# Modulation rows summed over features on VectorE and over partitions by a block of ones, in place of column-tiled products of the raw weights

## The chip, the cores and the metric

The kernel runs on one core of a Trainium2 chip. The metric is the device time of one execution in microseconds (us), as the median of three runs. The names of the engines in the rows are PE (TensorE, matrix products), PEld (its loads of the stationary operand), DVE (VectorE), ACT (ScalarE), POOL (GpSimd) and SP (SyncE, which here issues the transfers).

## The reference

Two networks run one behind the other on a sequence of 256 tokens of 1024 features. The first has two layers of three attention branches, which are merged by gates. The second has two layers as well, an even one (Fourier mixing and gated chunks, latent and context tokens) and an odd one (neighbourhood attention), each followed by a convolutional feed-forward network. All weights are fp32.

Only one piece of it is computed in another way by the change: the modulation rows of the second network. Two vectors, one for the latent tokens and one for the context, go through `silu` and are multiplied by a weight of 1024 x 6144 in each layer:

```python
s_lat = jax.nn.silu(c)
s_ctx = jax.nn.silu(c_ctx)
for layer in range(DEPTH):
    mod = (s_lat @ ada_w[layer] + ada_b[layer])[:, None, :]
    mod_c = s_ctx @ ada_w[layer] + ada_b[layer]
    sh1, sc1, g1, sh2, sc2, g2 = jnp.split(mod, N_MOD, axis=-1)
    csh1, csc1, cg1, csh2, csc2, cg2 = jnp.split(mod_c, N_MOD, axis=-1)
    h = modulate(x, norm1_g[layer], sh1, sc1)
    ...
    x = x + g1 * y
    x = x + g2 * conv_ffn(modulate(x, norm2_g[layer], sh2, sc2), ...)
```

In the last layer the context tokens are not carried on; there only the shift and scale of the first norm (the first two of the six parts) are used for the context.

## The kernel before

Weights come in pieces of 512 KB. `piece` (L163 to L176) loads one into a `raw` buffer by a transfer on SP's queue, ACT makes the upper half `whi` of each number (L173), and DVE the rest, `wlo` (L174). A product with a weight is three matmuls, upper by upper, upper by lower and lower by upper (`tok_target` L228 to L230, `feat_target` L238 to L240). The pieces go round in a ring of three raw buffers and seven pairs of halves (`rings = [(wp, 3, 7)]`).

Each engine works its instructions in one fixed order. A scheduler makes that order when the program is built, from modelled times, so the instructions of an engine don't stand there in the order of the source.

The modulation rows are made by a generator, `ada` (from L376), which the other stages call for a step at a time through `fill` (L181), two steps at once. There are two layers, six groups of 1024 columns in each, and eight steps `k` in a group. Each step loads a tile of 128 features x 1024 columns, `adaw`. It multiplies the tile as it is (raw fp32) by the two vectors `cs`, which are the stationary operand of 128 x 2: four products of 256 columns each, placed side by side in the array by `tile_position` (L392). The eight steps of a group add up in one PSUM bank. Then four DVE instructions of 2 x 256 add the bias (`adab`, L398), and four transfers write the rows to DRAM, into `modd`. The rows of layer 0 are made while the first network runs, those of layer 1 during the feed-forward network of layer 0. The last group of layer 1 is loaded at the end of the odd stage into buffers that are free by then (`adar`), multiplied at its end by `fill(1000)` (L1338), and its bias is added in the last feed-forward network. `load_mod` (L863) and `load_gates` (L873) fetch rows back from `modd`.

In the first network the large products have three PSUM banks, `ps_mm` with `turn = [None]`, since `ps_x` holds the fourth for the modulation sums; afterwards they have four.

Norms: `Row.rstd` (L299 to L315) makes the factor of a row, `xs` (L320) is the scaled row tile, `pT` its transposes on PE (L336), `hf` (L342, L346) applies the gain, and `hh` (L351) and `hl` (L353) are the halves that the next products read. At the boundary of the two layers of the first network the residual addition is `x_sb<-pw` (L778).

In the feed-forward network (`ffn`, from L1089) an iteration makes a tile of `pfg` (gate) and `pfv` (value), DVE makes `fg` from them (L1144), and `pfd` is the second product. `fill` is called once in every iteration there.

## Time and profile before

| what | us |
|---|---|
| median of three runs | 1633.25 (1631.62 to 1634.20) |
| profiled execution | 1632.92 |
| its span | 1631.0 |
| PE busy | 1603.7 (98%) |
| loads of the stationary operand | 1333.0 (82%) |
| DVE busy | 1035.2 (63%) |
| ACT busy | 797.5 (49%) |
| moved by transfers | 265.83 MB, mean 163 GB/s |

The profile is one execution, recorded by the hardware. Busy time is summed over the whole span, so a share says nothing of a single stage. Records of PE overlap: matmuls are pipelined and their ends are modelled. "Granted clock" is the share of TensorE's full clock that was given in a stretch. The chain of waits goes back from the last instruction, at each step to what released it or to the instruction ahead of it on its engine. An fp32 product leaves two records of matmuls, so a step of `ada` has eight of them.

### The profile page before, as it was taken

How to read it: one execution, taken by the hardware profiler on the slowest of the kernel's cores; microseconds unless marked ns; L12 is line 12 of the kernel's file. 1: busy time of each engine (PE TensorE's matmuls, PEld its weight loads, DVE VectorE, ACT ScalarE, POOL GpSimd, SP SyncE). 2: the span in 40 equal slices, each digit the busy share in tenths (PEclk: the TensorE clock that was granted, in tenths of full speed). 3: DMA queues.
4: the chain of work that ended last, by engine and by line, in shares of the span. 5: the costliest groups of instructions: out<-in, count | busy, mean ns of one | idle time of the engine just before them, and what ended most of it. 6: DMA issues, size and time to landing. Idle time of an engine off the chain costs nothing.

```text
span 1631.0 us, 25920 instructions
## 1 busy us (share of the span) xinstructions
PE 1603.7 (98%) x10017; PEld 1333.0 (82%) x10017; DVE 1035.2 (63%) x2133; ACT 797.5 (49%) x1353; POOL 29.7 (2%) x45
## 2 busy tenths in 40 slices
PE   7999999999999999999999999999999999999999
PEld 5878898977788989878897778777787777689897
DVE  6795556667866566785665553545448656688773
ACT  6465545455555455664363331333246554676451
POOL 0000000000000000000000000000000111100000
PEclk9999999999999999999999999999999999999999
DMA  7754565656655555542235562455424323566650
GB/s 270 234 182 145 197 222 175 202 200 207 205 163 188 195 182 169 165 149 83 73 104 181 181 188 85 161 176 173 125 78 134 101 59 117 184 223 229 221 168 27
DMA packets 79308, 265.83 MB, mean 163 GB/s; under 512 B 9744, under 2 KB 14672, under 8 KB 79184
## 3 DMA queue, kind: packets, MB, share of 16 engines
q1 hardware_dynamic: 79184, 264.17, 49.9%
q8 instruction: 79, 1.29, 0.3%
q14 instruction: 45, 0.37, 0.1%
HBM read 262.98 MB, written 1.15 MB: 162 GB/s over the span
## 4 chain that ended last, share of the span: by engine, by line
PE 89%; DVE 4%; DMA 3%; ACT 3%; issue 1%; SPq 0%; ACTq 0%; DVEq 0%
PE pfg L238 4%; PE pfg L240 4%; PE pfv L240 4%; PE pfg L239 4%; PE pfv L239 4%; PE pfv L238 4%; PE pfd L1162 4%; PE pfd L1164 4%; PE pfd L1163 4%; PE pmg L238 3%; PE pmg L240 3%; PE pmg L239 3%; PE pada L392 2%; DMA raw<-in_w_in 2%; DVE wlo L174 2%; PE poq L228 1%
## 5 line engine op out<-in xcount | busy, mean ns | idle before, releaser
L174 DVE TENSOR_TENSOR wlo<-raw,whi 128x1024 fp32r<-128x1024 f32 (+1 forms) x390 | 471.6, 1212 | 252.9 <-ACT whi L173 250.5
L173 ACT ACTIVATE whi<-raw 128x1024 fp32r<-128x1024 f32 (+1 forms) x390 | 406.9, 1049 | 408.3 <-PE pfd L1164 71.2
L238 PE MATMUL pfg<-hh,whi 128*128 128x256 f32 (+1 forms) x368 | 123.8, 337 | 1.9 <-ACT hh L351 1.9
L240 PE MATMUL pfg<-hh,wlo 128*128 128x256 f32 (+1 forms) x368 | 122.8, 334 | 0.0
L238 PE MATMUL pfv<-hh,whi 128*128 128x256 f32 (+1 forms) x368 | 121.5, 330 | 1.3 <-DVE fg L1144 1.3
L240 PE MATMUL pfv<-hh,wlo 128*128 128x256 f32 (+1 forms) x368 | 122.4, 333 | 0.0
L239 PE MATMUL pfg<-hl,whi 128*128 128x256 f32 (+1 forms) x368 | 121.9, 331 | 0.0
L239 PE MATMUL pfv<-hl,whi 128*128 128x256 f32 (+1 forms) x368 | 121.7, 331 | 0.0
L238 PE MATMUL pmg<-hh,whi 128*128 128x256 f32 x384 | 108.5, 282 | 0.0
L240 PE MATMUL pmg<-hh,wlo 128*128 128x256 f32 x384 | 107.6, 280 | 0.0
L239 PE MATMUL pmg<-hl,whi 128*128 128x256 f32 x384 | 107.6, 280 | 0.0
L1164 PE MATMUL pfd<-whi,gl 128*128 128x512 f32 (+1 forms) x275 | 105.8, 385 | 0.0
L1162 PE MATMUL pfd<-whi,gh 128*128 128x512 f32 (+1 forms) x275 | 105.7, 385 | 0.0
L1163 PE MATMUL pfd<-wlo,gh 128*128 128x512 f32 (+1 forms) x275 | 105.0, 382 | 0.0
L238 PEld LDWEIGHTS pfg<-hh,whi 128*128 128x128 f32 x368 | 69.6, 189 | 16.5 <-issue 3.9
L238 PEld LDWEIGHTS pfv<-hh,whi 128*128 128x128 f32 x368 | 69.2, 188 | 8.7 <-DVE fg L1144 1.5
L239 PEld LDWEIGHTS pfv<-hl,whi 128*128 128x128 f32 x368 | 69.6, 189 | 7.8
L239 PEld LDWEIGHTS pfg<-hl,whi 128*128 128x128 f32 x368 | 69.9, 190 | 7.2 <-DVE hl L353 0.2
L240 PEld LDWEIGHTS pfg<-hh,wlo 128*128 128x128 f32 x368 | 69.6, 189 | 7.0
L240 PEld LDWEIGHTS pfv<-hh,wlo 128*128 128x128 f32 x368 | 69.4, 188 | 7.0
L238 PEld LDWEIGHTS pmg<-hh,whi 128*128 128x128 f32 x384 | 72.2, 188 | 1.2 <-issue 1.2
L239 PEld LDWEIGHTS pmg<-hl,whi 128*128 128x128 f32 x384 | 72.2, 188 | 0.2 <-issue 0.2
(320 smaller groups left out, 3739.9 us busy)
## 6 DMA issues: line engine op xcount, KB each, us to landing
raw<-in_w_in SPq DMA_DIRECT2D x152, 512.0 KB
raw<-in_ffn_up SPq DMA_DIRECT2D x96, 512.0 KB
adaw<-in_ada_w SPq DMA_DIRECT2D x88, 512.0 KB
raw<-in_ffn_down SPq DMA_DIRECT2D x40, 512.0 KB
raw<-in_w_branch SPq DMA_DIRECT2D x24, 512.0 KB
raw<-in_odd_qkv SPq DMA_DIRECT2D x24, 512.0 KB
raw<-in_w_out SPq DMA_DIRECT2D x16, 512.0 KB
raw<-in_even_in SPq DMA_DIRECT2D x12, 512.0 KB
```

The costliest lines, as they stand in the source:

```text
L173: behind(ACT.activation(hi, raw, AF.Copy))
L174: behind((sub or DVE).tensor_sub(lo, raw, hi.bitcast(F32)))
L228: PE.matmul(ps, xh[:, k, tsl], hi, start=first, stop=False)
L238: PE.matmul(ps, hi[:, msl], xh[:, k, :], start=first, stop=False)
L239: PE.matmul(ps, hi[:, msl], xl[:, k, :], start=False, stop=False)
L240: PE.matmul(ps, lo[:, msl], xh[:, k, :], start=False, stop=last)
L392: PE.matmul(ps[32 * j:32 * j + 2, 0:256], cs[:, 2 * k:2 * k + 2], raw[:, j * 256:j * 256 + 256], start=k == 0, stop=k == KD - 1, tile_posi ...
L1162: PE.matmul(ps, gh[:, k, tsl], hi[:, i, csl], start=k == 0, stop=False)
L1163: PE.matmul(ps, gh[:, k, tsl], lo[:, i, csl], start=False, stop=False)
L1164: PE.matmul(ps, gl[:, k, tsl], hi[:, i, csl], start=False, stop=k == NH - 1)
```

## The change

Each step `k` no longer goes to PE. For each needed row `s`, DVE multiplies the whole tile of 128 x 1024 by the factor of each partition (`cs[:, 2k+s]`) and adds it to a sum `adaa`: a multiplication for k = 0, then seven multiply-adds. Two rows are made in layer 0 and in the first two groups of layer 1, one row in the other four. At a group's end PE adds the sum up over the partitions: the stationary operand is a block of 128 x 32 ones, the moving one is `adaa`, again in four column tiles of 256 columns, for each row. One DVE instruction adds the bias (`adar`, now spread over 32 partitions), and four transfers write the rows.

Counted over the program, DVE gets 20 multiplications and 140 multiply-adds of 128 x 1024 and 12 read-outs (eight of 128 x 512, four of 128 x 256), and loses 48 instructions of 2 x 256. On PE 96 groups of four products go, and 20 groups of four come, in 12 places (two groups in eight of them, one in four).

With it go: the separate bank (`ps_x`), so that the first network has the fourth bank as well; the preloaded last group of layer 1, which is now made in the feed-forward network of layer 0 like the others; one pair of the halves' buffers (seven to six); and `fill(2)` in the second half of that network becomes `fill(3)`.

```diff
-    turn = [None]
+    turn = [0]
...
-    rings = [(wp, 3, 7)]
+    rings = [(wp, 3, 6)]
...
+            rows_ = range(2 if layer == 0 or g < 2 else 1)
+            n = len(rows_)
+            acc = [pool.tile([P, 1024], F32, tag=f"adaa{s}", bufs=1, name=nm("adaa")) for s in rows_]
+            bias = pool.tile([P, 256], F32, tag="adab", bufs=1, name=nm("adab"))
             for j in range(4):
-                SP.dma_start(bias[32 * j:32 * j + 2, :],
-                             A["ada_b"][layer:layer + 1, s0 + j * 256:s0 + j * 256 + 256].broadcast_to([2, 256]))
-            ps = bank(nm("pada"))
+                SP.dma_start(bias[32 * j:32 * j + 32, :],
+                             A["ada_b"][layer:layer + 1, s0 + j * 256:s0 + j * 256 + 256].broadcast_to([32, 256]))
             for k in range(KD):
-                raw = ada_ahead.pop((g, k)) if (g, k) in ada_ahead else ada_load(layer, g, k)
-                for j in range(4):
-                    PE.matmul(ps[32 * j:32 * j + 2, 0:256], cs[:, 2 * k:2 * k + 2], raw[:, j * 256:j * 256 + 256],
-                              start=k == 0, stop=k == KD - 1, tile_position=(0, 32 * j))
+                raw = pool.tile([P, 1024], F32, tag="adaw", bufs=2, name=nm("adaw"))
+                SP.dma_start(raw, A["ada_w"][layer, g, :, k, :])
+                for s in rows_:
+                    c = cs[:, 2 * k + s:2 * k + s + 1]
+                    if k == 0:
+                        DVE.tensor_scalar_mul(acc[s], raw, c)
+                    else:
+                        DVE.scalar_tensor_tensor(acc[s], raw, c, acc[s], op0=ALU.mult, op1=ALU.add)
                 if k == KD - 1:
...
+                    ps = ps_tr(nm("pada"))
+                    for s in rows_:
                         for j in range(4):
+                            PE.matmul(ps[32 * j:32 * j + 32, s * 256:s * 256 + 256], C("ones", 0, 32),
+                                      acc[s][:, j * 256:j * 256 + 256], start=True, stop=True,
+                                      tile_position=(0, 32 * j))
+                    r = sp.tile([P, 2, 256], F32, tag="t512", bufs=4, name=nm("adar"))[:, 0:n, :]
+                    DVE.scalar_tensor_tensor(r, ps[:, 0:n * 256].rearrange("p (s c) -> p s c", s=n), 0.5,
+                                             bias.unsqueeze(1).broadcast_to([P, n, 256]), op0=ALU.mult, op1=ALU.add)
...
                 elif l == 0:
-                    fill(2)
+                    fill(3)
...
-        room = []
-        for tag in ("okT0", "okT1", "ov"):
-            r = po.tile([P, 2, 1024], F32, tag=tag, bufs=1, name=nm("adar"))
...
-        for k, r in enumerate(room):
-            ada_ahead[5, k] = ada_load(1, 5, k, r)
...
-        fill(1000)
```

On DVE at the start of the program, behind the first norm, stands before the change the following. `cs` are the vectors, `rope` and `qs` the turned heads, `wlo` a lower half of a weight.

```order
L812 SCALAR_TENSOR_TENSOR cs<-cs,vec 128x16
L423 TENSOR_TENSOR rope_284<-qs_282,cst 128x8x8
L424 TENSOR_TENSOR rope_284<-qs_282,cst 128x8x8
L425 TENSOR_TENSOR qs_282<-qs_282,cst 128x8x16
L426 TENSOR_TENSOR qs_282<-qs_282,rope_284 128x8x16
L174 TENSOR_TENSOR wlo_299<-raw_296,whi_298 128x1024
```

In the changed program the same place of DVE reads as follows.

```order
L804 SCALAR_TENSOR_TENSOR cs<-cs,vec 128x16
L383 TENSOR_SCALAR adaa_213<-adaw_220,cs 128x1024
L383 TENSOR_SCALAR adaa_214<-adaw_220,cs 128x1024
L385 SCALAR_TENSOR_TENSOR adaa_213<-adaw_224,cs,adaa_213 128x1024
L385 SCALAR_TENSOR_TENSOR adaa_214<-adaw_224,cs,adaa_214 128x1024
L415 TENSOR_TENSOR rope_281<-qs_279,cst 128x8x8
L416 TENSOR_TENSOR rope_281<-qs_279,cst 128x8x8
L171 TENSOR_TENSOR wlo_296<-raw_293,whi_295 128x1024
```

The first four sums stand ahead of the first `wlo` of the attention weights.

The next two pieces are DVE at the boundary of the two layers of the first network. Here `x_sb<-pw` is the residual addition of a row tile's half, `rsv`, `rsy` and `rst` the row factor, `xs` the scaled row. Before:

```order
L778 SCALAR_TENSOR_TENSOR x_sb<-pw_3814,x_sb 128x512
L309 SCALAR_TENSOR_TENSOR rsv_3868<-rss_3763,rsu_3764 128x1
L310 TENSOR_SCALAR rsv_3868<-rsv_3868 128x1
L174 TENSOR_TENSOR wlo_3863<-raw_3860,whi_3862 128x1024
L311 RECIPROCAL rsy_3870<-rsr_3869 128x1
L313 SCALAR_TENSOR_TENSOR rst_3871<-rsy_3870,rsv_3868 128x1
L314 SCALAR_TENSOR_TENSOR rsy_3870<-rst_3871,rsy_3870 128x1
L320 TENSOR_SCALAR xs_3878<-x_sb,rsy_3870 128x1024
L342 TENSOR_SCALAR hf_3881<-pT_3880,vec 128x128
L778 SCALAR_TENSOR_TENSOR x_sb<-pw_3904,x_sb 128x512
```

With the change, at the same boundary on DVE:

```order
L171 TENSOR_TENSOR wlo_3832<-raw_3829,whi_3831 128x1024
L306 SCALAR_TENSOR_TENSOR rsv_3837<-rss_3736,rsu_3737 128x1
L308 RECIPROCAL rsy_3839<-rsr_3838 128x1
L770 SCALAR_TENSOR_TENSOR x_sb<-pw_3873,x_sb 128x512
L307 TENSOR_SCALAR rsv_3837<-rsv_3837 128x1
L385 SCALAR_TENSOR_TENSOR adaa_3577<-adaw_4169,cs,adaa_3577 128x1024
L310 SCALAR_TENSOR_TENSOR rst_3840<-rsy_3839,rsv_3837 128x1
L306 SCALAR_TENSOR_TENSOR rsv_3901<-rss_3744,rsu_3745 128x1
L308 RECIPROCAL rsy_3903<-rsr_3902 128x1
L311 SCALAR_TENSOR_TENSOR rsy_3839<-rst_3840,rsy_3839 128x1
L307 TENSOR_SCALAR rsv_3901<-rsv_3901 128x1
L317 TENSOR_SCALAR xs_3847<-x_sb,rsy_3839 128x1024
```

The scaled row tile `xs` of the first row stood ahead of the last `x_sb<-pw`; now it stands behind it and behind a sum.

On PE, where the first attention scores (`psc`) begin, the order before has two steps of the modulation between a product and the scores:

```order
L229 MATMUL pq_979<-wlo_976,hh_90 128x512
L230 MATMUL pq_979<-whi_975,hl_91 128x512
L228 MATMUL pq_980<-whi_975,hh_90 128x512
L229 MATMUL pq_980<-wlo_976,hh_90 128x512
L230 MATMUL pq_980<-whi_975,hl_91 128x512
L392 MATMUL pada_218<-adaw_1043,cs 2x256 x4
L392 MATMUL pada_218<-adaw_1049,cs 2x256 x4
L499 MATMUL psc_1072<-qk_360 128x128
```

The same place of PE with the change:

```order
L225 MATMUL pq_969<-whi_964,hh_90 128x512
L226 MATMUL pq_969<-wlo_965,hh_90 128x512
L227 MATMUL pq_969<-whi_964,hl_91 128x512
L390 MATMUL pada_1040<-adaa_213,cst 32x256 x4
L390 MATMUL pada_1040<-adaa_214,cst 32x256 x4
L491 MATMUL psc_1064<-qk_357 128x128
```

It is the first visit of the modulation to PE in the changed program: the two row sums of group 0, where before it was one of several visits of group 0.

## Rows read from the trace of the kernel before

**Rows 1.** The page: busy time of the engines, DVE in 40 slices, chain by engine.
```profile
PE 1603.7 (98%) x10017; PEld 1333.0 (82%) x10017; DVE 1035.2 (63%) x2133; ACT 797.5 (49%) x1353; POOL 29.7 (2%) x45
...
DVE  6795556667866566785665553545448656688773
...
PE 89%; DVE 4%; DMA 3%; ACT 3%; issue 1%; SPq 0%; ACTq 0%; DVEq 0%
```

**Rows 2.** The chain of waits: start us, us, engine, name, line, count of records.
```profile
23.17 0.97 PE pada L392 x16
...
34.59 1.13 DVE wlo L174
...
392.00 1.14 DVE wlo L174
...
532.22 1.23 DVE wlo L174
...
879.74 0.98 PE pada L392 x16
892.11 0.97 PE pada L392 x16
```

**Rows 3.** Groups of PE and PEld by line and shape: busy us, mean ns | idle before.
```profile
L392 PE MATMUL pada<-adaw,cs 128*2 128x256 f32 x704 | 46.0, 379 | 0.0
...
L228 PEld LDWEIGHTS pq<-whi,hh 128*128 128x128 f32 x160 | 30.7, 192 | 8.7 <-issue 1.3 <-ACT hh L351 0.9
L392 PEld LDWEIGHTS pada<-adaw,cs 128*2 128x2 f32 x704 | 13.9, 83 | 22.3 <-issue 9.9 <-DMA raw<-in_w_in 0.7 <-DVE rope L424 0.4
```

**Rows 4.** Groups of DVE by line and shape, the same columns.
```profile
L174 DVE TENSOR_TENSOR wlo<-raw,whi 128x1024 fp32r<-128x1024 f32 x382 | 466.1, 1223 | 248.1 <-ACT whi L173 245.6 <-PE psg L1049 0.5
L398 DVE SCALAR_TENSOR_TENSOR adab<-pada,adab 2x256 f32<-2x256 f32 x48 | 20.1, 419 | 1.8 <-PE pada L392 0.8
...
L717 DVE SCALAR_TENSOR_TENSOR mth<-mth,py 128x512 f32<-128x512 f32 x16 | 10.9, 684 | 9.9 <-PE py L240 9.9
L320 DVE TENSOR_SCALAR xs<-x_sb,rsy 128x1024 f32<-128x1024 f32 x12 | 9.0, 754 | 0.4
L659 DVE MATCH_REPLACE8 wk<-m,wk 128x256 f32<-128x256 f32 x14 | 5.7, 408 | 0.0
L828 DVE SCALAR_TENSOR_TENSOR x_sb<-x_sb,rsy,fg 128x512 f32<-128x512 f32 x4 | 2.8, 749 | 0.1
```

**Rows 5.** Windows: us; PE, PEld, DVE, ACT, POOL busy; granted clock, DMA share, GB/s.
```profile
20.00:120.00 100.00, 98.84 (x586) 78.10 (x585) 80.95 (x215) 56.13 (x86) 0.00 (x0) 1.00 0.70 227
400.00:460.00 60.00, 59.38 (x370) 47.55 (x369) 50.66 (x139) 32.02 (x52) 0.00 (x0) 1.00 0.58 184
842.00:880.00 38.00, 38.00 (x239) 32.44 (x241) 22.73 (x27) 17.35 (x22) 0.00 (x0) 1.00 0.45 153
879.70:966.40 86.70, 86.70 (x453) 64.81 (x456) 46.32 (x60) 30.47 (x38) 0.00 (x0) 1.00 0.56 180
1039.50:1163.30 123.80, 123.80 (x645) 92.53 (x648) 63.16 (x80) 41.20 (x52) 0.00 (x0) 1.00 0.54 173
1437.00:1441.40 4.40, 4.07 (x20) 3.88 (x21) 3.12 (x6) 3.92 (x8) 0.00 (x0) 0.61 0.21 84
```

**Rows 6.** Timeline of PE at the boundary of the layers: start us, us, instruction.
```profile
353.21 0.40 PE L230 MATMUL pw<-whi,mh 128*128 128x512 f32 x1
...
354.97 0.50 PE L228 MATMUL pq<-whi,hh 128*128 128x512 f32 x1 [0.38 <-ACT hh L351]
```

**Rows 7.** Timeline of DVE at the same place.
```profile
351.24 0.75 DVE L320 TENSOR_SCALAR xs<-x_sb,rsy 128x1024 f32<-128x1024 f32 x1
...
353.92 0.68 DVE L778 SCALAR_TENSOR_TENSOR x_sb<-pw,x_sb 128x512 f32<-128x512 f32 x1
```

**Rows 8.** Timeline of PE behind the odd stage.
```profile
1434.34 1.06 PE L336 MATMUL pT<-cst,xs 128*128 128x128 f32 x8 [0.94 <-DVE xs L320]
1437.33 0.38 PE L238 MATMUL pfg<-hh,whi 128*128 128x256 f32 x1 [1.92 <-ACT hh L351]
```

## Prediction made before the changed kernel ran

> **What bounds the kernel now.** I read the page first. TensorE (PE) is busy 98% of the span, VectorE (DVE) 63%, and the chain of waits puts 89% of the span on PE and 4% on DVE [rows 1]. That says: time taken off PE comes off the end, unless the work that replaces it makes PE wait. The DVE line of the 40 slices shows where it could: mostly fives and sixes, but sevens, eights and a nine in slices 2 and 3 and at the end [rows 1]. Then I read the chain for the modulation products (L392). They stand in it 38 times, the first at 23.17 us, each visit of 16 matmul records (two k-tiles, four column tiles each, an fp32 product being two records) for 0.97 or 0.98 us, some for 1.02 [rows 2]; all visits together are 704 records, so 44 visits [rows 3]. These are visible stops of PE: in the feed-forward network of layer 0 one stands exactly every 12.37 us (879.74, then 892.11) [rows 2]. Last I read the windows of the places where the new DVE work will land, and there the idle of DVE: 19.05 of 100 us at 20 to 120, 9.34 of 60 us at 400 to 460, 15.27 of 38 us at 842 to 880 [rows 5].
>
> Times below are made against the profiled execution, 1632.92 us (span 1631.0). The median of the runs shown is 1633.25, 0.33 us more. Differences under 0.2%, 3.3 us, are about what a measurement of this kernel can tell from no change.
>
> **The change part by part.**
>
> *Taken from PE.* 38 visits on the chain at a mean of 0.975 us: 37.1 us. Six visits are not on the chain, worth 0 to 5.9 us; I take half, 2.9. The eight k-tiles of the last group, 64 records at 1428 to 1433 [rows 8], I count at nothing: the transposes of the next norm wait for `xs` behind them and the first `pfg` waits another 1.92 us for `hh` [rows 8], so DVE and ACT set the time there; were that cover gone, four more visits, 3.9 us, would be saved. Together -40.0.
>
> *Added to PE.* 20 products of four column tiles in 12 visits, eight with two rows (16 records) and four with one (8 records). The moving operand is again 128x256 in fp32, 379 ns a record, four column tiles side by side [rows 3]; the stationary one has 32 columns where it had 2. No row shows a 32-column load; the nearest are 83 ns for 2 columns and 192 ns for 128 [rows 3]. A visit of 16 records took 0.97 us, so by count 8x0.97 + 4x0.49 = 9.7 us. From above: 160 loads, each at 192 ns with no overlap, 30.7 us. From below the count stands: the same columns stream through as in the old visits, and nothing speaks for less. I take 9.7, as 32 columns lie nearer to 2 than to 128. Gross on PE: -30.3 (-6 to -33: the six visits left out and the loads in full, or the six counted in full).
>
> The Trainium skill ("TensorEngine Tiling (Array Packing)", Key Properties) says that changing the tiling mode drains TensorE, so that a price per visit would be right rather than one per product. By it the 12 visits would cost 12x0.97 = 11.7 instead of 9.7, 2 us more; no row here parts the two.
>
> *Added to DVE.* 20 multiplications and 140 multiply-adds of 128x1024 in fp32. The first kind is in the trace: 754 ns (`xs` L320) [rows 4]. The second is not at this width. The subtraction of the same shape with two sources takes 1223 ns; at 128x512 the multiply-add takes 749 (L828) and 684 (L717) ns [rows 4]. The dearer of these beside the cheaper gives 65 ns, so 1.288 us each (bounds 1.22 and 2x0.749 = 1.50). The 48 small `adab` instructions, 20.1 us, go [rows 4]; 12 read-outs of the ones products come, eight as long as the 128x512 of L717, 0.684 us, and four of half that width at 0.42, as long as an `adab` [rows 4]. Net: 15.1 + 180.3 + 7.2 - 20.1 = 182.5 us, DVE from 1035 to about 1218 us, 75% of the span. So DVE doesn't become the bound on the whole; it must be asked stretch by stretch. DVE works its instructions in the order in which they are written, so behind a sum stand the `wlo` halves that PE's products wait for.
>
> *Start, 20 to 120 us.* Ahead of the first attention output 21 sums now stand on DVE, four of them multiplications: 4x0.754 + 17x1.288 = 24.9 us. Two `wlo` (2.4 us), about eight selection instructions at 0.408 us (3.3) [rows 4] and about 1 us of `adab` left this stretch in exchange: net 18.2 against 19.05 us of idle [rows 5]. That is almost all of the idle, and some of it lies where DVE waits for a copy on ACT that in its turn waits for a transfer, hence is not free to use. Here the chain runs through `wlo` eight times, from 34.59 us on [rows 2]: PE is already waiting for DVE. Cost 0 to 18; I take 6, a third, because the scheduler puts the sums between the `wlo`, not in a block, while eight links of 1.1 to 1.2 us show that about a third of the added time can push directly.
>
> *Layer boundary, 352 us.* Before, the first row tile's `xs` (351.24) is done ahead of the last residual addition (353.92), so the transposes and the first `pq` of layer 1 are under way 1.4 us after the last `pw` product ended (353.61, `pq` at 354.97) [rows 6, 7]. In the new order of DVE two `wlo`, the last residual addition and one sum stand ahead of that `xs`. Then after the last `pw` come the addition 0.69, the sum 1.29, the small operations of the row factor (my estimate: 1.2, as `rsv` to `xs` is a chain of seven on columns of 128x1), `xs` 0.75, and as before some 3 us from `xs` to `pq` (351.24 + 0.75 to 354.97) [rows 6, 7]: 6.9 us instead of 1.4. That is 5.5 us. PE lost clock after an idle stretch before: at 1437 to 1441.4, behind the wait for `hh` [rows 8], the granted clock was 0.61 [rows 5], between its two levels of 0.5 (1.2 GHz) and 1 (2.4 GHz); 39% of 4.4 us is 1.7 more. I take 7 (3 if other PE work is in hand, 10).
>
> *Dense stretch of layer 1, 400 to 460 us.* 14 sums stand in it, 18.0 us, against 9.34 us of idle [rows 5]; but no link of the chain there is a DVE one (after the `wlo` at 392.00 the next in it is at 532.22 [rows 2]), so PE has work in hand. 0 to 8.7; I take 2.
>
> *Feed-forward network of layer 0.* 16 sums stand ahead of the fourth iteration's `fg`: 20.6 us against 15.27 us idle in 842 to 880 [rows 5], 5.3 short. Later in the first half an iteration has 46.32/7 = 6.6 us of DVE [rows 5], and four sums make 11.8, beside 12.37 - 0.97 = 11.40 us for PE. The `adab` share of 0.4 us in the 6.6 goes, so they are level. 0 to 5; I take 2. The second half has three sums in an iteration, 63.16/10 + 3.9 = 10.2 against 11.4 [rows 5]: nothing.
>
> *The rest.* Seven to six buffers for the weight halves, a fourth bank in block 1, stages that start 30 us of PE earlier with the same weights to load (DMA share 0.70 in the densest stretch [rows 5]), and the last group's sums in the feed-forward network instead of before the last one: 0, within 2 either way.
>
> Sum: -40.0 + 9.7 + 6 + 7 + 2 + 2 = -13.3, so 1619.6 us for the profiled execution, 1620 as median.
>
> **The rivals.**
>
> *All sums are covered.* DVE is idle 37% of the span [rows 1], and it is enough if the sums slip into gaps. Then the net is -27 to -33 and the time 1600 to 1606. For it: only 15 `wlo` links in block 1 are on the chain. Against it: the boundary, where the order itself puts `xs` behind a sum.
>
> *The sums block the weight halves (slower).* The mechanism is the order on DVE: a sum stands ahead of a `wlo` or `xs` that PE needs, and the idle before it was a wait for a copy or a transfer, which a queue can't use for something written further back. Then the idle of the dense stretches is worth nothing: 18 + 10 + 8.7 + 5 = 41.7 us come back, -30.3 + 41.7 = +11.4, 1645 us. It decides from 30.3 us of returned time, that is if three quarters of the overlap fails. For it: 248 us of DVE's idle is a wait for `whi` [rows 4]. Against: 38 of the 44 removed stops are real, and from 120 to 350 us DVE shows five and six tenths. The Trainium skill ("TensorE: Matmul & The Clock Gate", Architectural detail: the array is 16× 32×32, not 1× 128×128) calls VectorE's queue strict FIFO, which speaks for this rival; what it would make of the time is the 1645 of this paragraph, and the trace of before, with DVE on 4% of the chain, doesn't yet bear it out.
>
> *The products don't get cheaper.* If the ones products cost the upper 30.7 us, PE gains only 9.3, and with the same 17 us paid back the time is 1641. Against it: 16 records took under 1 us in a visit.
>
> **How the numbers follow.** Forecast with its neighbours (1606 to 1628): 0.45. All covered (1598 to 1606): 0.21. Between, within 0.2%, 1630 to 1636.5: 0.13 (this holds half of a partly blocked queue). Slower, by the queue or by the dear products: 0.21, of which half beyond 1642. So faster 0.66, same 0.13, slower 0.21. The range goes from 1602, which leaves half of the covered case below it, 0.1, to 1642, which leaves 0.1 above.
>
> **What would show it right or wrong.** After: 160 sums of about 1.29 us and 0.75 us, and 12 visits of at most 1 us on PE, no longer one per 12.37 us iteration; the iteration of the feed-forward network at 11.4 us. DVE busy near 1218 us. At the boundary of the layers `xs` behind the last `x_sb` addition, PE idle for 5 to 7 us with a lower granted clock after it. In 20 to 120 us more `wlo` links in the chain than eight. The forecast is wrong if PE's idle before `whi`/`wlo` products grows by more than 30 us in all, or if the iteration doesn't shrink because DVE's `fg` now ends last.

## The result and the profile after

The changed kernel takes 1610.78 us (median of four, 1609.79 to 1613.74) beside 1633.72 of the kernel before on the same chip: a ratio of 0.9862, with an interval of 0.9848 to 0.9877. Run once more, beside others, it gave 1611.32 us and 0.9868 (0.9853 to 0.9883). So it is 21 to 23 us faster; the forecast was 1620 us, in a range of 1602 to 1642. The profiled execution took 1610.21 us (span 1608.1).

The page of after, in the parts that answer to [rows 1]; the second line is DVE in 40 slices:

```profile
PE 1570.2 (98%) x9409; PEld 1328.9 (83%) x9409; DVE 1185.1 (74%) x2257; ACT 798.9 (50%) x1353; POOL 29.4 (2%) x45
...
DVE  7999668787987856876679784578558656688773
...
PE 85%; DVE 7%; DMA 4%; ACT 2%; issue 1%; SPq 0%; DVEq 0%; ACTq 0%
```

PE still carries the chain, but DVE's share went from 4% to 7%. The slices show where DVE filled up: slices 2 to 4, from 40 us on, are at 90% and more, where [rows 1] has 7, 9 and 5.

The answers for the tiles `adaa` and `pada` of after (count; shortest, median and longest ns; first and last start):

```profile
L385 DVE SCALAR_TENSOR_TENSOR adaa<-adaw,cs,adaa x140: 1251/1279/1287, 24.1 to 1131.2; 128x1024 f32<-128x1024 f32 x140
L383 DVE TENSOR_SCALAR adaa<-adaw,cs x20: 723/746/757, 22.8 to 1108.8; 128x1024 f32<-128x1024 f32 x20
...
L390 PEld LDWEIGHTS pada<-adaa,cst x160: 106/109/110, 103.1 to 1132.7; 128*32 128x32 f32 x160
```

A multiply-add takes 1.279 us (forecast 1.288), a multiplication 0.746 (0.754), and a load of 32 columns 109 ns, between the 83 and 192 of [rows 3].

The next table shows when the same matmul starts in the traces (us; the runs of the last four columns are told below; the traces of e2_short and e3_bound are of executions of 1603.72 and 1603.71 us, the shortest of theirs):

| matmul | before | after | e8_hybrid | e3_bound | e2_short | e10_split |
|---|---|---|---|---|---|---|
| first `ppT` (attention, layer 0) | 102.8 | 105.0 | 100.9 | 102.8 | 100.8 | 103.8 |
| 48th `pw` (end of layer 0) | 339.8 | 336.5 | 337.2 | 332.9 | 332.7 | 337.8 |
| 27th `psm` (start of layer 1) | 367.4 | 371.4 | 366.4 | 362.8 | 365.3 | 367.7 |
| first `pev` (second network) | 692.3 | 690.6 | 689.3 | 684.2 | 682.7 | 694.9 |
| first `pfg` (feed-forward, layer 0) | 830.6 | 827.5 | 826.3 | 821.2 | 820.0 | 831.8 |
| first `poq` (odd stage) | 1226.9 | 1205.5 | 1206.1 | 1199.1 | 1198.8 | 1210.2 |

The whole first network, with 24 of the 44 removed visits, gained 1.7 us (692.3 to 690.6). That is within what single executions differ by: a second trace of the changed kernel (e4_after_again) starts the first `pev` at 692.0, and the two traces of it already stand at 13.2 and 11.7 us at the ninth `pT`, ahead of the first sum (22.8 us). The feed-forward network of layer 0, with the other 20 visits, takes 396.3 us before (first `pfg` to first `poq`) and 378.0 in both traces of the changed kernel: 18.3 us gained (from 3.1 to 21.4 us ahead).

The other 2.9 us are 1.4 in the even stage and 1.5 in the last feed-forward network, most of them two waits of PE that the trace of before has and that of after has not:

```profile
722.79 0.50 PE L238 MATMUL pef<-hh,whi 128*128 128x512 f32 x1 [1.16 <-DVE vn L992]
...
1475.47 0.39 PE L238 MATMUL pfv<-hh,whi 128*128 128x256 f32 x1 [1.25 <-DVE fg L1144]
```

It doesn't take the new sums to lose them: e5_ring6, which is the kernel before with six pairs of the halves' buffers, has neither wait, though it keeps all products and every `adab`.

**The price of a visit.** The timeline of PE around one visit in the feed-forward network, before and then after (start us, us, instruction, count of records):

```profile
903.86 0.39 PE L239 MATMUL pfv<-hl,whi 128*128 128x512 f32 x1
904.09 0.40 PE L240 MATMUL pfv<-hh,wlo 128*128 128x512 f32 x1
904.42 1.05 PE L392 MATMUL pada<-adaw,cs 128*2 128x256 f32 x16
905.39 0.50 PE L238 MATMUL pfg<-hh,whi 128*128 128x512 f32 x1
905.73 0.39 PE L239 MATMUL pfg<-hl,whi 128*128 128x512 f32 x1
```

```profile
897.17 0.40 PE L237 MATMUL pfv<-hh,wlo 128*128 128x512 f32 x1
897.50 1.07 PE L390 MATMUL pada<-adaa,cst 128*32 128x256 f32 x16
898.50 0.50 PE L235 MATMUL pfg<-hh,whi 128*128 128x512 f32 x1
898.84 0.40 PE L236 MATMUL pfg<-hl,whi 128*128 128x512 f32 x1
...
1107.55 0.40 PE L237 MATMUL pfv<-hh,wlo 128*128 128x512 f32 x1
1107.87 0.64 PE L390 MATMUL pada<-adaa,cst 128*32 128x256 f32 x8
1108.44 0.50 PE L235 MATMUL pfg<-hh,whi 128*128 128x512 f32 x1
1108.78 0.39 PE L236 MATMUL pfg<-hl,whi 128*128 128x512 f32 x1
```

Matmuls of 512 columns start 0.23 us apart (903.86, 904.09). The visit starts 0.33 us after the one ahead of it, and the second matmul behind starts 0.34 after the first. From 904.09 to 905.73 are 1.64 us; two matmuls alone would be 0.47. So a visit costs 1.17 us, not the 0.97 of its own row in the chain. With two rows after it is 1.67 - 0.47 = 1.20, with one row 1.235 - 0.467 = 0.77: the two differ by one product, 0.43, and 0.34 is left for the visit itself. An iteration, 12.37 us before, is 11.2 now (46.0 us from the visit at 897.50 to that at 943.50 are four of them and one visit; the prediction's sign was 11.4).

**Covered in the feed-forward network.** Windows of after (us; busy PE, PEld, DVE, ACT, POOL; granted clock, DMA share, GB/s), first one in the feed-forward network, then the two places of the first network where PE waited:

```profile
898.80:943.30 44.50, 44.50 (x192) 35.66 (x190) 39.49 (x44) 15.12 (x19) 0.00 (x0) 1.00 0.58 184
...
80.00:90.00 10.00, 7.42 (x37) 5.23 (x36) 9.86 (x27) 7.27 (x10) 0.00 (x0) 0.74 0.71 226
340.00:362.00 22.00, 14.55 (x59) 11.59 (x58) 16.86 (x32) 11.90 (x29) 1.07 (x3) 0.77 0.56 186
```

With DVE busy for 39.5 of 44.5 us, 89%, PE didn't stop at all. At 80 to 90 us DVE is full (9.86 of 10 us) and PE stands for 2.6 us. At 340 to 362 us DVE is busy for less of the time than in the feed-forward network, 77%, and PE stands for 7 us. So how full DVE is doesn't decide it alone; what stands behind a sum in its queue does as well.

**The clock behind the waits.** Behind the waits for `pix` (2.58 us, told below) and for `xs` (6.88 us, in the next part) the granted clock falls. Two windows of after with the same columns, then the starts of PE in the second of them:

```profile
84.80:95.00 10.20, 9.41 (x27) 6.68 (x28) 8.30 (x28) 4.78 (x11) 0.00 (x0) 0.50 0.49 160
351.10:361.20 10.10, 5.65 (x21) 4.72 (x22) 7.62 (x21) 5.21 (x15) 0.34 (x1) 0.50 0.48 157
...
359.28 0.63 PE L227 MATMUL pq<-whi,hl 128*128 128x512 f32 x1
359.71 0.63 PE L225 MATMUL pq<-whi,hh 128*128 128x512 f32 x1
```

A share of 0.50 is the lower of the two levels, 1.2 GHz, and matmuls start 0.43 us apart there instead of 0.23. With 3.3 us more at 433 us PE was busy at it for 18.4 us, so by an estimate from these rows some 8 us of the first network are lost to the clock. From 15 to 692 us the kernel before and e8_hybrid have 1.00.

**The boundary of the layers.** DVE, then PE, in the timeline of after; the bracket is the idle time ahead of an instruction and what ended it:

```profile
348.26 1.28 DVE L385 SCALAR_TENSOR_TENSOR adaa<-adaw,cs,adaa 128x1024 f32<-128x1024 f32 x1 [2.06 <-DMA adaw<-in_ada_w]
349.47 2.35 DVE L171 TENSOR_TENSOR wlo<-raw,whi 128x1024 fp32r<-128x1024 f32 x2
...
351.88 0.67 DVE L770 SCALAR_TENSOR_TENSOR x_sb<-pw,x_sb 128x512 f32<-128x512 f32 x1
...
352.53 1.28 DVE L385 SCALAR_TENSOR_TENSOR adaa<-adaw,cs,adaa 128x1024 f32<-128x1024 f32 x1
...
354.17 0.75 DVE L317 TENSOR_SCALAR xs<-x_sb,rsy 128x1024 f32<-128x1024 f32 x1
```

```profile
347.70 0.40 PE L227 MATMUL pw<-whi,mh 128*128 128x512 f32 x1
354.98 1.97 PE L333 MATMUL pT<-cst,xs 128*128 128x128 f32 x8 [6.88 <-DVE xs L317]
...
358.28 0.78 PE L225 MATMUL pq<-whi,hh 128*128 128x512 f32 x1
```

A sum waits 2.06 us for its tile's transfer, and behind it in the queue stand two `wlo`, the last residual addition, another sum and the `xs` for which PE waits 6.88 us. The transfer is in the chain of waits (start us, us, what):

```profile
343.17 5.00 DMA adaw<-in_ada_w
```

It starts just as an earlier sum has ended (at 343.15) and takes 5.00 us; the tiles have two buffers, which fits a transfer that waits for one of them. From the last `pw` (ends 348.10) to the first `pq` it is 10.2 us, where [rows 6] has 1.4.

### The profile page after: what moved, and what is told of

The parts are those of the page before. It is cut to its first block, busy times and chain, and to the rows that moved or that the text cites. A ratio compares the mean times of both kernels' runs of the same rounds, so it can differ in the third digit from the quotient of the medians.

```text
span 1608.1 us, 24865 instructions
## 1 busy us (share of the span) xinstructions
PE 1570.2 (98%) x9409; PEld 1328.9 (83%) x9409; DVE 1185.1 (74%) x2257; ACT 798.9 (50%) x1353; POOL 29.4 (2%) x45
## 3 DMA queue, kind: packets, MB, share of 16 engines
HBM read 264.45 MB, written 1.13 MB: 165 GB/s over the span
## 4 chain that ended last, share of the span: by engine, by line
PE 85%; DVE 7%; DMA 4%; ACT 2%; issue 1%; SPq 0%; DVEq 0%; ACTq 0%
PE pfg L235 4%; PE pfg L237 4%; PE pfv L237 4%; PE pfv L236 4%; PE pfv L235 4%; PE pfg L236 4%; PE pfd L1153 4%; PE pfd L1152 4%; PE pfd L1151 4%; DVE wlo L171 3%; PE pmg L235 2%; PE pmg L236 2%; PE pmg L237 2%; PE poq L225 1%; DMA raw<-in_w_in 1%; PE poq L227 1%
## 5 line engine op out<-in xcount | busy, mean ns | idle before, releaser
L170 ACT ACTIVATE whi<-raw 128x1024 fp32r<-128x1024 f32 x390 | 408.2, 1050 | 415.5 <-PE pfd L1153 78.7
L171 DVE TENSOR_TENSOR wlo<-raw,whi 128x1024 fp32r<-128x1024 f32 x390 | 470.7, 1211 | 162.5 <-ACT whi L170 159.5
L385 DVE SCALAR_TENSOR_TENSOR adaa<-adaw,cs,adaa 128x1024 f32<-128x1024 f32 x140 | 176.9, 1278 | 19.1 <-DMA adaw<-in_ada_w 19.1
```

The costliest lines, as they stand in the source:

```text
L170: behind(ACT.activation(hi, raw, AF.Copy))
L171: behind((sub or DVE).tensor_sub(lo, raw, hi.bitcast(F32)))
L385: DVE.scalar_tensor_tensor(acc[s], raw, c, acc[s], op0=ALU.mult, op1=ALU.add)
```

## The experiments

**Is a visit's price its products?** e1_half leaves half of the column tiles out of the kernel before.

```diff
-                for j in range(4):
+                for j in range(2):
                     PE.matmul(ps[32 * j:32 * j + 2, 0:256], cs[:, 2 * k:2 * k + 2], ...
...
```

> The kernel before, with two of the four column tiles of every modulation product left out (columns 512 to 1023 of a group are not computed, their rows get other columns' sums). All 44 visits of PE and all loads of weights stay. Theory: a visit is worth 1.17 us, of which 0.97 is its 16 matmul records and 0.2 the matmul ahead of it and behind it, which start 0.1 us later than usual. Half of the records then takes 0.48 us from each of 44 visits, 21 us: about 1612, and the iteration of the feed-forward network goes from 12.37 to 11.89 us. Rival: the four column tiles run side by side and the price is the switch into another tiling, so half of the records costs nearly the same: within 3 us of 1633, iteration 12.3.

Measured: 1632.35 us, ratio 1.0009 (0.9998 to 1.002). The theory as I put it fell. The visit in the timeline of e1_half:

```profile
903.02 1.03 PE L392 MATMUL pada<-adaw,cs 128*2 128x256 f32 x8
903.98 0.50 PE L238 MATMUL pfg<-hh,whi 128*128 128x512 f32 x1
```

8 records take 0.96 us, as 16 did. So the four column tiles run side by side, and leaving two of them out saves nothing. But that doesn't yet make the price one of the switch: each column tile still has its four records, one behind the other. What grows with the number of steps could not be told from this run.

**Price of the visit or of the steps?** e7_four asks for the same products four steps at a time.

```diff
-    rings = [(wp, 3, 7)]
+    rings = [(wp, 3, 6)]
...
-        if owed[0] < 2:
+        if owed[0] < 4:
...
-            raw = ada_pool[0].tile([P, 1024], F32, tag="adaw", bufs=2, name=nm("adaw"))
+            raw = ada_pool[0].tile([P, 1024], F32, tag="adaw", bufs=4, name=nm("adaw"))
```

> The kernel before, with its modulation steps asked for four at a time instead of two (four buffers for their tiles, paid with one of the seven pairs of the halves): all products stay, in 22 visits instead of 44, apart from the last group. Theory: a visit costs 0.34 us for itself (the matmul ahead and behind start late) and 0.43 for each step, so 22 visits less are 7.5 us: 1623 to 1626. Rival one: the whole 1.17 us is the price of a visit, 22 of them are 26 us: 1605 to 1608. Rival two: the visit itself is free, the price is the products: 1630 to 1634.

Measured: 1623.22 us beside 1632.58, 0.9941 (0.9926 to 0.9956): 9.4 us. Its chain, with the start, length and records of a visit:

```profile
897.90 1.84 PE pada L392 x32
```

Two visits of 0.97 became one of 1.84, and one pair of late neighbours went with it: 2x1.17 - (1.84 + 0.20) = 0.30 us for each visit saved, 6.6 for 22. That is the theory's mechanism, and in the feed-forward network the trace has it: ten visits fewer take 392.9 us from the first `pfg` to the first `poq`, where e5_ring6 (below), with six pairs too, takes 395.9. The other 2.8 us of the measured 9.4 (the interval is about 2.5 to either side) are not assigned for certain; the six pairs alone take away the waits at 722.79 and 1475.47 us. Both rivals are out.

**Is it the smaller ring?** e5_ring6 is the kernel before with six pairs.

```diff
-    rings = [(wp, 3, 7)]
+    rings = [(wp, 3, 6)]
```

> The kernel before, with six instead of seven pairs of buffers for the weight halves and nothing else. Theory: the halves are not what PE waits for, so nothing: 1631 to 1636. Rival: a part of what the changed kernel paid back in the first network is the missing pair: 1638 to 1650.

Measured: 1631.22 us beside 1631.92, 0.9993 (0.9983 to 1.0002). As a whole the missing pair costs nothing. In its trace it is not without effect: the two waits named above are gone, and the boundary of the layers (48th `pw` to 27th `psm`) takes 29.2 us instead of 27.6, as it does in e8_hybrid.

**What did the first network bring?** e8_hybrid keeps the products on PE for layer 0 of the modulation and takes the sums for layer 1.

```diff
-    turn = [0]
+    turn = [None]
...
-        filler[0] = ada(0)
+        filler[0] = ada_pe(0, ps_x)
...
```

> The changed kernel, with the modulation of layer 0, made in the first network, as it was before (products of the raw tiles on PE, its own bank, three banks for the others); layer 1, made in the feed-forward network, by sums on DVE. Theory: in the feed-forward network the sums are covered, 20 visits at 1.17 go and six at 1.2 or 0.77 come, 18 us, and 1.5 more behind the odd stage; the first network brings nearly nothing net, so this kernel has nearly all of the gain: 1611 to 1614. Rival: each removed visit brings the same wherever it stood, so 24 of 44 are lost: 1619 to 1623.

Measured: 1610.87 us, 0.9867 (0.9852 to 0.9882); the changed kernel on the same chip had 1611.32:

> The changed kernel once more, unaltered, on the chip of the runs beside it: 1608 to 1614 by every theory, so that the others have it as their measure.

The two are the same. Everything that 96 of the 160 sums took off PE in the first network was paid back there; the gain is that of the feed-forward network, with the 2 to 3 us of the two waits. The table has it too: e8_hybrid enters the second network at 689.3 us, the changed kernel at 690.6 (692.0 in its second trace), e5_ring6, without any sums, at 690.3. In the feed-forward network e8_hybrid gains 16.5 us and not 18.3, since there the last ones product does wait for its sum:

```profile
1133.19 0.64 PE L393 MATMUL pada<-adaa,cst 128*32 128x256 f32 x8 [1.69 <-DVE adaa L388]
```

**What is it paid with?** e2_short shortens the multiply-adds to 8 columns and leaves their waits.

```diff
-                        DVE.scalar_tensor_tensor(acc[s], raw, c, acc[s], op0=ALU.mult, op1=ALU.add)
+                        DVE.scalar_tensor_tensor(acc[s][:, 0:8], raw[:, 0:8], c, acc[s][:, 0:8], op0=ALU.mult, op1=ALU.add)
```

> The changed kernel, with the 140 multiply-adds cut to 8 of 1024 columns (the modulation rows are wrong beyond them); each still waits for its tile's transfer, the 20 first multiplications, the ones products and all transfers stay. Theory: of 39 us that PE gained about 19 were paid back in the first network by the time of the sums on DVE, 8.4 of them at the boundary of its layers. Without their duration 14 to 18 come back (the wait for a tile's transfer of 2 us at the boundary may stay): 1593 to 1597. Rival: the sums are covered by idle of DVE, and what was paid back comes from the six buffers, the bank or the new visits: 1608 to 1612.

Measured: 1604.38 us, 0.9832 (0.9817 to 0.9846): 5 to 6 us faster than the changed kernel, where the theory said 14 to 18 and its rival nothing. At the first `ppT` 4.2 us came back (105.0 to 100.8), or 1.2 against the second trace of the changed kernel (102.0): that is duration, and the wait for `pix` at 85 us is 0.60 us as before, with no half clock behind it. At the boundary a wait is left, since in e2_short (DVE, then PE) stands:

```profile
341.13 0.36 DVE L385 SCALAR_TENSOR_TENSOR adaa<-adaw,cs,adaa 128x8 f32<-128x8 f32 x2 [2.11 <-DMA adaw<-in_ada_w]
341.41 0.68 DVE L770 SCALAR_TENSOR_TENSOR x_sb<-pw,x_sb 128x512 f32<-128x512 f32 x1
```

```profile
347.50 1.09 PE L333 MATMUL pT<-cst,xs 128*128 128x128 f32 x8 [3.21 <-DVE xs L317]
350.43 0.80 PE L225 MATMUL pq<-whi,hh 128*128 128x512 f32 x1 [1.83 <-ACT hh L348]
```

Two short sums, 0.36 us together, still hold a residual addition for 2.11 us, until their tile has landed. And PE waits 1.83 us for `hh`: in the kernel before a visit (353.54) stood just there, in a pause that was there anyway. So the visit at the boundary was free, and its removal brought nothing. So the 5 to 6 us are what the duration of the sums costs, with the clock behind it; the waits for tiles stay in this run and are not priced apart by it.

**The boundary alone.** e3_bound asks for no steps there and for more in the second layer.

```diff
...
+            more[0] = 1.0 if l else 0.0
             run(merge(0))
             branch(2, r2, merge(1))
+            more[0] = 0.0
...
+            mute[0] = l == 0
             run(merge(2))
...
         layer(0, hT, done0)
-        fill(1)
+        mute[0] = False
```

> The changed kernel, with no modulation steps asked for in the last merge and the output product of the first layer; as many more are asked for in the merges of the second layer. By the order on DVE no sum then stands between the last residual addition of the first layer and its norm, and the first row's scaled tile stands ahead of that addition again. Theory: the wait of PE of 6.9 us for the scaled tile and the half clock behind it go, 7 to 9 us: 1602 to 1604. Rival: the 12 moved sums push the weight halves of the second layer by as much: 1609 to 1612.

Measured: 1608.08 us, 0.9847 (0.9828 to 0.9865), and, with more rounds,

> The kernel that asks for no modulation steps around the boundary of the first network's layers, once more with more rounds, since its first measurement (ratio 0.9847, interval 0.9828 to 0.9865) overlaps that of the changed kernel (0.9862 and 0.9868). Theory: 5 us of the boundary stay gained: a ratio of 0.983 to 0.985, clear of the changed kernel. Rival: what goes at the boundary comes back in the second layer, where the moved sums stand: 0.986 to 0.988, no difference.

1607.41 us, 0.9837 (0.9814 to 0.9859). PE at the boundary of e3_bound:

```profile
345.03 1.09 PE L341 MATMUL pT<-cst,xs 128*128 128x128 f32 x8 [0.54 <-DVE xs L325]
...
347.95 0.53 PE L233 MATMUL pq<-whi,hh 128*128 128x512 f32 x1 [1.83 <-ACT hh L356]
```

The wait for `xs` is 0.54 us instead of 6.88. From the 48th `pw` to the 27th `psm` it is 29.9 us, as against 34.9 after, 27.6 before and 29.2 in e5_ring6: 5 of 7.3 us came back, and 1.83 for `hh` with the clock behind it stayed. Of the 2.3 us that stayed, 1.6 are there with six pairs and no sums as well. Against the changed kernel the medians stand 3 to 4 us lower, but the intervals overlap; I take it as probably the better kernel, not as shown.

**Moved out of the dense starts too.** e4_placed mutes the first four projections of both layers as well, and asks for more behind them.

```diff
+            mute[0] = True
             r0, steps = project(0)
...
+            mute[0] = False
+            more[0] = 0.5 if l == 0 else 1.0
             r1, steps = project(1)
```

> The changed kernel, with no modulation steps asked for in the last merge and output product of the first layer, and none in the first four projections of either layer of the first network (where the index selection fills DVE); the others there ask for one and a half or two. Theory: what the sums cost is set by where they stand, in the dense stretches and at the boundary; moved to where DVE has idle, at least 8 of the 19 us come back: 1600 to 1603. Rival: the sums only change places, the stretches that take them are then the dense ones: 1606 to 1611.

Measured: 1607.57 us, 0.9857 (0.9835 to 0.988): within the rival's 1606 to 1611, no better than e3_bound. Fewer steps asked for in the first projections don't keep the sums from there: 16 still stand ahead of the first attention output, where the changed kernel has 21, since the scheduler, which goes by its modelled times, still places them there.

**Held back by force.** e10_split makes the groups 0 to 2 of layer 0 on PE and holds the sums of groups 3 to 5 behind the first scores of the second layer.

```diff
...
-                        DVE.scalar_tensor_tensor(acc[s], raw, c, acc[s], op0=ALU.mult, op1=ALU.add)
+                        gated(DVE.scalar_tensor_tensor(acc[s], raw, c, acc[s], op0=ALU.mult, op1=ALU.add))
...
-        filler[0] = ada(0)
+        filler[0] = ada_pe(0, ps_x, range(3))
...
+        filler[0] = ada(0, range(3, 6))
...
```

> A kernel meant to beat both: layer 1 of the modulation by sums on DVE in the feed-forward network, as in the changed kernel; of layer 0 the groups 0 to 2 as products on PE during the first layer of the first network (one visit of them stands at its boundary, where PE has to wait for the norm anyway), the groups 3 to 5 by sums on DVE that are held behind the first scores of the second layer, past its dense stretch. Theory: against the hybrid run (1610.9) 12 visits at 1.17 go and 3 at 1.2 come, 10.4 us, and up to 3 are paid back, since DVE is half idle there: 1600 to 1604. Rival: in the first network sums are never covered, wherever they stand, and the gain is paid back as before: 1608 to 1612.

Measured: 1614.77 us, 0.9884 (0.9866 to 0.9903): above even what the rival said. The theory's gain isn't there. The median is 3.9 us above the hybrid's, which ran on another chip, and the intervals overlap; so it is probably worse than the hybrid, which the times alone don't show. Up to the second layer it is within 1.3 us of the hybrid; the loss is between there and the second network (from 0.3 us behind the kernel before to 2.6 behind, though where nine visits stood in that stretch there are three). Two stretches of its chain of waits (start us, us, engine, name, line):

```profile
467.41 2.39 DVE adaa L405 x2
469.80 1.20 DVE qk L499 x2
471.55 0.34 DVE o L589
...
478.28 2.39 DVE adaa L405 x2
...
481.01 1.14 DVE wlo L183
482.20 4.74 DMA raw<-in_w_in
487.02 1.06 ACT whi L182
488.08 0.39 ACT pT L574
```

Pairs of sums, 2.39 us, stand ahead of the copies `qk` and the product `o` on which the attention's next step on PE waits; and a `wlo` that comes late frees its `raw` buffer late, so that the next transfer (482.20) and the copies on ACT behind it are late. In the kernel before DVE is busy for 23.3 of the 40 us from 460 to 500, in this one for 37.5: the held sums come in a crowd, and PE, which doesn't stop there before, is idle for 4.0 us. So this run doesn't say whether the same sums, spread out, would be covered.

**Fewer visits in the hybrid.** e11_hybrid4 is e8_hybrid with four steps at a time in the first network.

```diff
+    least = [4]
...
-        if owed[0] < 2:
+        if owed[0] < least[0]:
...
```

> The hybrid kernel, with the products of layer 0 asked for four steps at a time instead of two (four tile buffers): 12 visits of PE fewer, no sum more on DVE. Theory: each visit has a price of its own of 0.34 us, so 4.1 us: 1606 to 1608 against 1610.9. Rival: what the run with four at a time gained beside the kernel before came from the deeper prefetch in the feed-forward network, so nothing here: 1610 to 1612.

Measured: 1609.2 us, 0.9859 (0.9835 to 0.9884). The theory's 4 us are not shown by this, nor excluded: the interval reaches from 1605 to 1613. By position in the two traces it is 2.6 us ahead of the hybrid at the first `poq` (1203.5 to 1206.1), but only 0.8 of that in the first network (first `pev` at 688.5 and 689.3), where the two differ. The traces show where some 3.4 us of the theory's 4.1 are offset there: 0.8 at 12 us, ahead of the first visit (PE waits 2.86 us for `hf` as against 2.07); 0.86 by a wait for `cumz` at 48.9 us that the hybrid doesn't have; and 1.7 at the boundary of the layers, 30.9 us from the 48th `pw` to the 27th `psm` as against 29.2.

**How much does the feed-forward network cover?** e9_double issues each multiply-add of layer 1 twice.

```diff
+                        if layer == 1:
+                            DVE.scalar_tensor_tensor(acc[s], raw, c, acc[s], op0=ALU.mult, op1=ALU.max)
                         DVE.scalar_tensor_tensor(acc[s], raw, c, acc[s], op0=ALU.mult, op1=ALU.add)
```

> The changed kernel, with every sum of layer 1 issued twice (the extra one takes a maximum, so these rows are wrong): 54 more multiply-adds of 1.28 us in the feed-forward network, 69 us on DVE. Theory: the sums there are covered only as long as DVE's work in an iteration stays under PE's 11.2 us. It is 39.5 of 44.5 us now where two rows are summed, 9.9 in an iteration; doubled it is about 15, 4 us over in each of some five iterations, and in the second half 8.6 and three more sums, 12.4, 1.2 over in each of some eight: 25 to 35 us slower than the changed kernel, 1636 to 1646. Rival: DVE runs ahead of PE over the whole stage and the extra sums find room in the down products, where it has little to do: under 10 us, 1611 to 1620.

One execution: 1640.84 us, 30 more than the changed kernel, inside the theory's 1636 to 1646. By position in the two traces 25 of them are in the feed-forward network (403.0 us from the first `pfg` to the first `poq`, as against 378.0), the lower end of the theory's 25 to 35; 5 are in the first network, which the edit doesn't touch. The window and the waits of PE in it (total us, times, longest):

```profile
880.00:980.00 100.00, 86.18 (x360) 65.56 (x359) 94.16 (x98) 25.94 (x33) 0.00 (x0) 0.91 0.42 132
```

```profile
PE pada L392 <- DVE adaa L387: 8.5, 4, 4.3
PE pfv L235 <- DVE fg L1135: 2.8, 1, 2.8
```

Here DVE is full (94%) and PE waits: for the ones products, which now come before the sum is ready, and for `fg`. So the cover ends somewhere between the 89% of DVE that the changed kernel uses and this, as far as one execution shows it.

## Why the prediction was right, and where it was off

The direction, the bound and the kind of repayment were right; the time lay 9 us above the measured one. That it came no further off is in part luck, as terms with a wrong reason had about the right size. By its steps:

- *What bounds the kernel.* Right: PE, and the gain is time off PE.
- *Taken from PE.* The term was mis-sized. The chain's 0.97 us is a visit's own row; the visit starts 0.1 us late behind the matmul ahead of it, and the second matmul behind it another 0.1. The chain of before, asked for a window, has these 0.2 us in the `pfg` behind a visit (the row below, 0.43 us, where other `pfg` have 0.23). 1.17 for 44 visits is 51.5 instead of the 40.0 counted. But not each one was worth it: the visit at the boundary stood in a pause, as e2_short and e3_bound show. Of the first network as a whole e8_hybrid's equality says only that nothing was left net; it doesn't part visits that were worth nothing from gains that waits ate. The eight steps behind the odd stage, counted at nothing, were worth nothing: at the last `popT` and after the `pfg` that follows it the lead is 21.4 and 21.3 us.

```profile
880.72 0.43 PE pfg L238
```

- *Added to PE.* 9.7 us were counted; with 1.20 and 0.77 it is 8x1.20 + 4x0.77 = 12.7. The rows now part the two prices: 0.34 us go with each visit and 0.43 with each product, so neither price alone is right. The Trainium skill's rule that a change of the tiling mode drains TensorE ("TensorEngine Tiling (Array Packing)", Key Properties), from which the prediction estimated 11.7, agrees with the traces in that a part goes with each visit (e7_four saved it); that this part is the drain, no run here shows. The loads of 32 columns are 109 ns instead of 83 and lengthen a visit of 16 records by 0.03 us (1.00 to the next start instead of 0.97).
- Net of these two, -39 where the forecast had -30.3, if each visit counted.
- *Added to DVE.* The duration of each sum was right within about 1%. The total was not: 1185 us instead of 1218, because instructions that follow each other at once overlap in the records (two `wlo` are 2.35 us together, 1.22 each alone).
- *Start.* 6 us forecast. Between 80 and 95 us the changed kernel went from 3.7 us ahead to 2.2 behind, 5.8 us; in its second trace it is 3.6. The size was about right, by luck, since the mechanism wasn't: the chain has eight `wlo` between 20 and 120 us as before, where more were named as a sign. PE didn't wait for a `wlo` but 2.58 us for `pix` (0.61 before), whose relu on ACT stands behind a `whi` that waits 1.88 us for DVE's index selection, which stands behind the sums. That is 2 of the 5.8 us, and the rest is the half clock of the 10 us behind it, which the forecast priced at the boundary alone.

```profile
85.59 2.56 PE L634 MATMUL pix<-qki 64*128 64x256 f32 x8 [2.58 <-ACT r L638]
```

- *Boundary.* 7 us forecast, 7.3 measured (3.3 us ahead at the 48th `pw`, 4.0 behind at the 27th `psm`). Place, order and the half clock behind the pause were right. Missed were the wait of a sum for its transfer, that the removed visit had been free, and that 1.6 of the 7.3 us come with six pairs without any sum (e5_ring6, e8_hybrid); that the size fits so well is luck.
- *Dense stretch of layer 1.* 2 us forecast, 2.8 measured at 430 us (4.2 in the second trace), again behind the relu of `pix` (PE waits 1.13 us ahead of `psc`) and with the half clock. A wait of 1.9 us for the attention output at 260 us, about 2 us in all, was not foreseen.
- *Feed-forward network.* 2 us forecast, 0 measured. Here the removed visits brought their full 1.17 us: 20x1.17 - 2x1.20 - 4x0.77 = 17.9, against 18.3 in the table. By the forecast's terms it was 20x0.975 - 3.9 - 2 = 13.6, so 4.7 of the 9 us by which it was off lie here; 2.9 are the next point, and some 2 the first network, where by its terms the repayment just ate the gain and 1.7 us were left (0.3 in the second trace, so that this part is within what executions differ by).
- *The rest.* 0 forecast, within 2; 1.5 us were gained around 1475 us and 1.4 in the even stage. Both go with the six pairs: the waits of before at 722.79 and 1475.47 us are missing in e5_ring6 and e7_four too, which keep the products and every `adab`, and the even stage (first `pev` to first `pfg`) takes 136.9 to 137.3 us in the kernels with six pairs and 138.3 and 138.5 in those with seven (before, e1_half). Why the missing pair takes these waits away is open.
- *The rivals.* The queue that blocks was the right mechanism for the first network: there nearly all came back. It was wrong for the feed-forward network. The Trainium skill's strict FIFO ("TensorE: Matmul & The Clock Gate", Architectural detail: the array is 16× 32×32, not 1× 128×128) agrees with the boundary's rows, where a sum waiting for a transfer holds the five instructions shown behind it. "All covered" came nearest in the total (1600 to 1606) and was wrong in its reason, as only a part of the kernel was covered, but at a higher price for each visit.

What stays open: a version that is clear of both kernels. e3_bound's medians are 3 to 4 us below the changed kernel, its interval overlaps. And why six pairs of buffers lose 1.6 us at the boundary and gain about as much in two other places.

## What to carry to other kernels

The price of a short visit to another kind of matmul is read from the starts of its neighbours, not from its own row: here 0.2 of 1.17 us lay outside it. Work moved to an engine with idle time was free where that engine runs ahead of the others (the feed-forward network, at 89% busy), and wasn't where the others wait for its short steps in turn (a norm at a boundary, at 77% busy; attention, where the moved sums filled it to 94%). A wait that the moved work makes can cost more than its own length, where the clock falls behind it (2 us of wait and 3.8 of clock at 85 us). Before moving work, ask for each stage which instruction will stand behind it in the queue, and for what the new instruction itself has to wait.

## What the runs showed of the hardware

- Four column tiles run side by side to the full: with two of the four left out a visit takes 0.96 us instead of 0.97 (e1_half).
- A visit of column-tiled matmuls between ordinary ones of 512 columns costs about 0.3 us of its own: 0.34 by visits of 8 and 16 records, 0.3 by visits of 16 and 32.
- Directly following instructions of DVE overlap by about 0.1 us in the records, so its busy time grows by less than the sum of what is added (150 us where the sum of all durations grows by 180).
- After a wait of PE of 2.58 us for `pix` and one of 6.88 us for `xs` the granted clock was 0.50 for 10.2 us each; after the 0.61 us wait for `pix` in the kernel before it stayed at 1.00.
